# MLP borders of a two-layer decoder: elementwise work on VectorE in place of GpSimd, and other PSUM banks for early products

## The chip, the cores and the metric

The kernel runs on one core of a Trainium2 chip. Five engines of the core work side by side, each through its own instructions in a fixed order: TensorE (PE in the rows; PEld is its weight load), VectorE (DVE), ScalarE (ACT), GpSimd (POOL) and SyncE (SP), which here only issues DMAs. They wait for each other through semaphores. The metric is the device time of one execution in microseconds (us), lower is better.

## The reference

Two layers of a decoder on x of 1024 tokens by 1024 features, all in float32. A layer has three residual steps; the third, the MLP, is the one at issue:

```python
def rms_norm(x, g):
    y = x * lax.rsqrt(jnp.mean(x * x, axis=-1, keepdims=True) + NORM_EPS)
    return y * g

for l in range(2):
    h = rms_norm(x, norm_mix_pre[l])
    ...                       # four mixers side by side, then w_out
    x = x + rms_norm(mixed, norm_mix_post[l])
    xa = cross_attention(rms_norm(x, norm_xa_pre[l]), ...)
    x = x + rms_norm(xa, norm_xa_post[l])
    hid = jnp.square(jax.nn.relu(rms_norm(x, norm_mlp_pre[l]) @ mlp_w1[l]))   # 1024 -> 4096
    x = x + rms_norm(hid @ mlp_w2[l], norm_mlp_post[l])                       # 4096 -> 1024
```

## The kernel before, in words

**Float32 products in three passes.** An operand is split into a high part (ScalarE's cast, L197) and the rest (VectorE's subtraction, L198): `wh`/`wl` and `hT` for the first matrix, `ao`/`bo` for the second, from raw tiles `wraw`, `araw` and `braw` that DMAs bring. A product is then three matmuls, L210 to L212 or L246 to L248. So each operand goes through ScalarE and VectorE once before TensorE can use it.

**Seven products in place of eight.** Both MLP products are cut into blocks of two by two and use a scheme of Strassen's kind: seven block products on sums and differences of blocks. For the first matrix the weights' sums S1 to S4 are made by L1471 to L1474 on GpSimd, and the tokens' sums T1 to T4 in `mlp_turn`, which transposes the normed tiles 4 to 7 (the tiles of the second half of the tokens) and subtracts or adds the transposes of tiles 0 to 3, as high and low parts: L1416 and L1425 (VectorE) take the high part, L1417 and L1426 (GpSimd) the low part. T-sums of the second matrix's blocks are made in `sums` (L1630 to L1639, GpSimd).

**First matrix.** Sixteen groups g of weights. `p1` and `p2` are a group's first two products; those of g = 0, 1, 2 need tiles 0 to 3 only and are run early, among the tail of cross attention (L309 adds its output to x, from a PSUM bank) and `mlp_turn`. `group` then runs the other products (and p1, p2 of the later groups), adds them up (L1531 to L1544, from PSUM, L1535 on GpSimd) and applies relu squared (L1499). The hidden blocks go to DRAM and come back as `araw`.

**Second matrix.** Blocks b = 0 to 4 of the hidden dimension. For b = 0 to 3 the seven products are added to accumulators `acc` (L1731 for b = 0, L1733 after it, four each), and in b = 3 `fold` adds accumulators to each other (L1670, 14 instructions a layer on GpSimd), which ends the scheme. Two orders of the products differ in where the folds come: after b = 3's P2, P5, P7 and P3. The last block is done as plain products by token tile (L1753); `part` takes the sum of squares (L1682, ScalarE) and multiplies by the norm's gain (L1683, GpSimd); `row` sums the squares (L1688), takes the power (`rstd`, L255 and L256 on GpSimd) and adds the row to the residual x (L1692). In the first layer the next layer's norm follows tile by tile (L275, L277, transposes L287); in the last layer this is the end of the kernel.

**What orders the work.** The functions are generators that are interleaved by hand; every engine runs its instructions in program order, and a tile's buffer is given to the next tile of its tag only when its last reader is done. PSUM has three pools: d (2 banks), u (4) and r (2).

Of the kernel before, what the change touches and what calls it, by code (L numbers as in the profile page):

```python
# [86 lines left out]
class Kern:  # L87
# [1303 lines left out]
    def mlp_turn(self, xs, tt, pst, X):  # L1391

        V, A, P, T = self.nc.vector, self.nc.scalar, self.nc.gpsimd, self.nc.tensor
        cs = slice(128 * (tt % 4), 128 * (tt % 4) + 128)
        if tt == 4:
            pair = lambda tag: [tuple(self.slot(tag, (128, 2, 512), F32R, name="hT") for _ in range(2)) for _ in range(2)]
            X[1] = {name: pair(tag) for name, tag in (("B22", "h"), ("T1", "h"), ("T2", "r"), ("T3", "r"), ("T4", "r"))}
        x = X[1]
        pt = []
        for b in range(2):  # L1400
            pt.append(self.psum(pst, (128, 4, 128), "pt"))
            for j in range(4):
                k = 4 * b + j
                T.transpose(pt[b][:, j, :], xs[:, k * 128:(k + 1) * 128], self.ident)
        b12, b22 = pt
        f, t2 = (xs[:, 512 * i:512 * i + 512].rearrange("p (k c) -> p k c", k=4) for i in range(2))
        two = lambda t, j: t[:, 2 * j:2 * j + 2]
        low = [tuple(t[:, :, cs] for t in X[0][j]) for j in range(4)]

        def split(name, src):  # L1410
            for j in range(2):
                h, lo = (t[:, :, cs] for t in x[name][j])
                self.split(h, lo, two(src, j))

        for j in range(2):
            V.tensor_tensor(two(f, j), two(b12, j), low[j][0], ALU.subtract)  # L1416
            P.tensor_tensor(two(f, j), two(f, j), low[j][1], ALU.subtract)  # L1417
        split("B22", b22)
        V.tensor_tensor(t2, b22, f, ALU.subtract)
        split("T1", f)  # L1420
        A.copy(f, b12)
        V.tensor_tensor(f, b22, f, ALU.subtract)
        split("T2", t2)
        for j in range(2):
            V.tensor_tensor(two(t2, j), low[2 + j][0], two(t2, j), ALU.subtract)  # L1425
            P.tensor_tensor(two(t2, j), two(t2, j), low[2 + j][1], ALU.add)  # L1426
        split("T3", f)
        split("T4", t2)

    def mlp(self, l, hT, gpost, gpre, xin, xout, dst, nxt):  # L1430
# [24 lines left out]
        def weights(g, raw=None):  # L1455

            if raw is None:
                raw = [self.slot("wr", name="wraw") for _ in range(2)]
                for i in range(2):
                    self.dma(raw[i], W[l, 2 * g + i])  # L1460
                yield
            if g not in ops:
                ops[g] = dict(zip(("A11", "A12"), pair(raw[0])))
            if g:
                yield
            o = ops[g]
            b = self.slot(("wh", "wl")[g % 2], (128, 2, 512), F32R, name="wb")
            self.split(b[:, 0], b[:, 1], raw[1][:, 512:1024])
            o["A22"] = tuple(b[:, i].rearrange("p (k c) -> p k c", k=4) for i in range(2))
            (a11, a12), (a21, a22) = ((r[:, 0:512], r[:, 512:1024]) for r in raw)  # L1470
            P.tensor_tensor(a22, a21, a22, ALU.add)  # L1471
            P.tensor_tensor(a21, a11, a21, ALU.subtract)  # L1472
            P.tensor_tensor(a11, a22, a11, ALU.subtract)
            P.tensor_tensor(a12, a12, a11, ALU.subtract)  # L1474
            yield
            yield
            o["S3"], o["S1"] = pair(raw[1])
            yield
            o["S2"], o["S4"] = pair(raw[0])
            yield  # L1480

        def product(g, tag, w, x):
            (wh, wl), xs = ops[g][w], X[x]
            ps = self.psum(tag)
            for k in range(4):
                xh, xl = xs[k // 2]
                self.mm3(ps, wh[:, k], wl[:, k], xh[:, k % 2], xl[:, k % 2], k == 0, k == 3)
                yield
            return ps
# [10 lines left out]

        def p1(g):
            s = gs[g] = dict(A=two("r", "ma"))
            ps = yield from product(g, "d", "A11", "B11")
            A.copy(s["A"][:, 0], ps)

        def p2(g):
            s = gs[g]
            s["B"] = two("g" if g < 2 else "x", "mb")
            ps = yield from product(g, "d", "A12", "B21")
            V.tensor_tensor(s["B"][:, 0], ps, s["A"][:, 0], ALU.add)  # L1510
            sq(s["B"][:, 0], g < NE)

# [110 lines left out]

        def sums(b, name):

            for u in range(len(blocks[b])):
                r = lambda n: rawB[b, n][u]
                if name == "T2":
                    b11, b12, b22 = (r(n) for n in ("B11", "B12", "B22"))
                    P.tensor_tensor(b11, b12, b11, ALU.subtract)  # L1630
                    rawB.setdefault((b, "T1"), []).append(b11)
                    t = self.slot("g", name="t2")
                    P.tensor_tensor(t, b22, b11, ALU.subtract)
                elif name == "T3":
                    t = r("B12")
                    P.tensor_tensor(t, r("B22"), t, ALU.subtract)
                else:
                    t = r("B21")
                    P.tensor_tensor(t, t, r("T2"), ALU.subtract)  # L1639
                rawB.setdefault((b, name), []).append(t)  # L1640

        def ahead():
# [24 lines left out]
        def fold(*pairs):  # L1667
            for to, of in pairs:
                for k in range(2):
                    P.tensor_tensor(acc[to][k], acc[to][k], acc[of][k], ALU.add)  # L1670

        folds = {"P2": (("P2", "P1"), ("P6", "P1")), "P5": (("P5", "P6"), ("P4", "P6")), "P7": (("P3", "P5"),),
                 "P3": (("P5", "P7"), ("P4", "P7"))}
# [3 lines left out]
        def part(tt, c, t, pst="d"):  # L1677

            if tt not in ssq:
                ssq[tt] = self.small([128, 2], "ssm", 5)  # L1680
            jk = self.psum(pst, name="junk")
            A.activation(jk, t, AF.Square, scale=D ** -0.5, accum_out=ssq[tt][:, c:c + 1])  # L1682
            P.tensor_tensor(t, t, gp[:, halves[c]], ALU.mult)  # L1683

        def row(tt, x):
            ss = ssq[tt]
            s1 = self.small([128, 1], "ssq", 3)
            V.scalar_tensor_tensor(s1, ss[:, 0:1], EPS, ss[:, 1:2], ALU.add, ALU.add)  # L1688
            r = self.rstd(s1)
            for p, sl in zip((("P2", "P3"), ("P4", "P5"))[tt // 4], halves):  # L1690
                t = y(p, tt % 4)
                V.scalar_tensor_tensor(x[:, sl], t, r, x[:, sl], ALU.mult, ALU.add)  # L1692
                if last and tt >= NT - 2:
                    self.dma(xout[tt][:, sl], x[:, sl])
            if not (last and tt >= NT - 2):
                self.dma(xout[tt], x)
            if not last:
                late.append((self.scaled(x, gn), tt))
# [321 lines left out]
```

## Time and profile before

| | us |
|---|---|
| three runs | 3330.42, 3341.13, 3345.55 (median 3341.13) |
| profiled execution, device time | 3333.72 |
| its span in the trace | 3331.9 |

The profiled execution granted TensorE 0.968 of its clock in the mean. The rows below are from this one execution, so its own time, 3333.72 us, is what sums of durations are held against. Rows of a timeline have the start in us from the span's start, the duration, engine, line, operation, output and inputs, and in brackets the idle time ahead of it on its engine with what ended it; "x2" stands for two like instructions in a row, whose durations are then taken together.

### The profile page before, as it was taken

How to read it: one execution, taken by the hardware profiler on the slowest of the kernel's cores; microseconds unless marked ns; L12 is line 12 of the kernel's file. 1: busy time of each engine (PE TensorE's matmuls, PEld its weight loads, DVE VectorE, ACT ScalarE, POOL GpSimd, SP SyncE). 2: the span in 40 equal slices, each digit the busy share in tenths (PEclk: the TensorE clock that was granted, in tenths of full speed). 3: DMA queues.
4: the chain of work that ended last, by engine and by line, in shares of the span. 5: the costliest groups of instructions: out<-in, count | busy, mean ns of one | idle time of the engine just before them, and what ended most of it. 6: DMA issues, size and time to landing. Idle time of an engine off the chain costs nothing. (4 is left out here: it accounts for less than half of the span.)

```text
span 3331.9 us, 46885 instructions
## 1 busy us (share of the span) xinstructions
PE 3150.6 (95%) x17696; PEld 2539.5 (76%) x17696; DVE 2085.0 (63%) x3316; ACT 1305.9 (39%) x2404; POOL 998.5 (30%) x762
## 2 busy tenths in 40 slices
PE   8999999999989998999799999899999899989997
PEld 6767777878867886887677777778788778878876
DVE  4457568364466667789634765673644676677894
ACT  5344444343443223433333454433434432234332
POOL 1000122010016776337410002110100168763374
PEclk9989999999999999999999999888999999999998
DMA  4323473252333445544333324622523334445433
GB/s 173 112 71 93 118 206 105 77 186 76 102 115 120 152 152 182 190 147 130 122 120 107 108 90 115 182 93 88 172 74 104 114 119 158 153 181 184 150 124 114
DMA packets 230850, 431.40 MB, mean 129 GB/s; under 512 B 59968, under 2 KB 109248, under 8 KB 230624
## 3 DMA queue, kind: packets, MB, share of 16 engines
q1 hardware_dynamic: 223968, 411.42, 37.3%
q0 software_dynamic: 6656, 16.98, 2.0%
q8 instruction: 140, 2.29, 0.3%
q14 instruction: 86, 0.70, 0.1%
HBM read 296.61 MB, written 131.69 MB: 129 GB/s over the span
## 5 line engine op out<-in xcount | busy, mean ns | idle before, releaser
L210 PE MATMUL p<-hT,wh 128*128 128x512 f32 x1536 | 616.4, 401 | 18.9 <-DVE x L309 10.7
L212 PE MATMUL p<-hT,wl 128*128 128x512 f32 x1536 | 606.2, 395 | 8.1 <-DVE wl L198 7.9
L211 PE MATMUL p<-hT,wh 128*128 128x512 f32 x1536 | 606.2, 395 | 0.0
L198 DVE TENSOR_TENSOR wl<-wraw,wh 128x1024 fp32r<-128x1024 f32 (+1 forms) x230 | 282.1, 1227 | 348.6 <-ACT wh L197 347.7
L197 ACT CAST wh<-wraw 128x1024 fp32r<-128x1024 f32 (+1 forms) x230 | 240.0, 1044 | 487.6 <-POOL wraw L1472 182.3
L246 PE MATMUL p<-bo,ao 128*128 128x512 f32 x912 | 361.1, 396 | 39.8 <-DVE mb L1544 25.1
L210 PEld LDWEIGHTS p<-hT,wh 128*128 128x128 f32 x1536 | 292.0, 190 | 95.2 <-issue 12.3
L247 PE MATMUL p<-bo,ao 128*128 128x512 f32 x912 | 358.7, 393 | 0.0
L248 PE MATMUL p<-bo,ao 128*128 128x512 f32 x912 | 358.5, 393 | 0.1
L212 PEld LDWEIGHTS p<-hT,wl 128*128 128x128 f32 x1536 | 291.3, 190 | 76.1 <-DVE wl L198 15.0
L211 PEld LDWEIGHTS p<-hT,wh 128*128 128x128 f32 x1536 | 292.0, 190 | 57.6 <-issue 0.7
L246 PEld LDWEIGHTS p<-bo,ao 128*128 128x128 f32 x912 | 174.0, 191 | 79.6 <-DVE mb L1544 26.0
L198 DVE TENSOR_TENSOR ao<-araw,ao 128x1024 fp32r<-128x1024 f32 x106 | 194.2, 1834 | 24.6 <-ACT ao L197 24.6
L246 PE MATMUL p<-wh,mt 128*128 128x512 f32 x512 | 204.2, 399 | 1.4 <-ACT junk L301 0.9
L248 PEld LDWEIGHTS p<-bo,ao 128*128 128x128 f32 x912 | 173.4, 190 | 37.7 <-DVE bo L198 0.9
L247 PEld LDWEIGHTS p<-bo,ao 128*128 128x128 f32 x912 | 173.9, 191 | 35.9
L248 PE MATMUL p<-wl,mt 128*128 128x512 f32 x512 | 200.9, 393 | 0.3 <-DVE wl L198 0.3
L247 PE MATMUL p<-wh,mt 128*128 128x512 f32 x512 | 200.9, 393 | 0.0
L198 DVE TENSOR_TENSOR bo<-braw,bo 128x1024 fp32r<-128x1024 f32 x92 | 158.6, 1726 | 59.0 <-ACT bo L197 49.7
L197 ACT CAST bo<-braw 128x1024 fp32r<-128x1024 f32 x92 | 96.1, 1050 | 224.1 <-PE p L247 128.0
L256 POOL TENSOR_TENSOR rs<-ssq,neghalf 128x1 f32<-128x1 f32 x48 | 27.1, 564 | 519.2 <-DVE ssq L303 508.9
L197 ACT CAST ao<-araw 128x1024 fp32r<-128x1024 f32 x106 | 110.9, 1050 | 88.9 <-DMA araw<-hd 88.3
(385 smaller groups left out, 6485.7 us busy)
## 6 DMA issues: line engine op xcount, KB each, us to landing
araw<-hd SPq DMA_DIRECT2D x106, 512.0 KB, 4.0
x<-x SPq DMA_DIRECT2D x80, 512.0 KB, 3.4
wraw<-in_mlp_w SPq DMA_DIRECT2D x68, 512.0 KB, 3.5
braw<-in_mlp_w SPq DMA_DIRECT2D x64, 512.0 KB, 4.8
wraw<-in_w_fm SPq DMA_DIRECT2D x32, 512.0 KB, 3.8
pj<-spl SPq DMA_DIRECT2D x64, 256.0 KB, 2.0
hd<-mb SPq DMA_DIRECT2D x64, 256.0 KB, 2.5
hd<-mc SPq DMA_DIRECT2D x64, 256.0 KB, 2.0
```

The costliest lines, as they stand in the source:

```text
L197: self.nc.scalar.copy(h, src)
L198: self.nc.vector.tensor_tensor(lo, src, h, ALU.subtract)
L210: mm(ps, wh, xl, start=first, stop=False)
L211: mm(ps, wh, xh, start=False, stop=False)
L212: mm(ps, wl, xh, start=False, stop=last)
L246: mm(ps, xl, wh, start=first, stop=False)
L247: mm(ps, xh, wh, start=False, stop=False)
L248: mm(ps, xh, wl, start=False, stop=last)
L256: P.tensor_tensor(r, ss, self.neghalf[:, 0:k], ALU.pow)
```

## The change

Six edits in the MLP, all of them about who does a step or where its result lies:

1. In `mlp_turn` L1417 and L1426 (the low parts) go from GpSimd to VectorE.
2. The weights' block sums L1471 to L1474 go to VectorE for group 0; the other fifteen groups keep GpSimd.
3. In `sums` the T-sums of block b = 0 of the second matrix go to VectorE; b = 1 to 3 keep GpSimd.
4. The folds go to VectorE.
5. `part` no longer multiplies by the gain. `row` multiplies y by the rstd and the gain in one VectorE instruction, and adds it to x in a second one.
6. p1 and p2 of the groups g = 0, 1, 2 take their PSUM banks from pool u rather than from d.

```diff
--- before.py
+++ after.py
@@ -1414,7 +1414,7 @@
 
         for j in range(2):
             V.tensor_tensor(two(f, j), two(b12, j), low[j][0], ALU.subtract)
-            P.tensor_tensor(two(f, j), two(f, j), low[j][1], ALU.subtract)
+            V.tensor_tensor(two(f, j), two(f, j), low[j][1], ALU.subtract)
         split("B22", b22)
         V.tensor_tensor(t2, b22, f, ALU.subtract)
         split("T1", f)
@@ -1423,7 +1423,7 @@
         split("T2", t2)
         for j in range(2):
             V.tensor_tensor(two(t2, j), low[2 + j][0], two(t2, j), ALU.subtract)
-            P.tensor_tensor(two(t2, j), two(t2, j), low[2 + j][1], ALU.add)
+            V.tensor_tensor(two(t2, j), two(t2, j), low[2 + j][1], ALU.add)
         split("T3", f)
         split("T4", t2)
 
@@ -1468,10 +1468,11 @@
             self.split(b[:, 0], b[:, 1], raw[1][:, 512:1024])
             o["A22"] = tuple(b[:, i].rearrange("p (k c) -> p k c", k=4) for i in range(2))
             (a11, a12), (a21, a22) = ((r[:, 0:512], r[:, 512:1024]) for r in raw)
-            P.tensor_tensor(a22, a21, a22, ALU.add)
-            P.tensor_tensor(a21, a11, a21, ALU.subtract)
-            P.tensor_tensor(a11, a22, a11, ALU.subtract)
-            P.tensor_tensor(a12, a12, a11, ALU.subtract)
+            E = P if g else V
+            E.tensor_tensor(a22, a21, a22, ALU.add)
+            E.tensor_tensor(a21, a11, a21, ALU.subtract)
+            E.tensor_tensor(a11, a22, a11, ALU.subtract)
+            E.tensor_tensor(a12, a12, a11, ALU.subtract)
             yield
             yield
             o["S3"], o["S1"] = pair(raw[1])
@@ -1500,13 +1501,13 @@
 
         def p1(g):
             s = gs[g] = dict(A=two("r", "ma"))
-            ps = yield from product(g, "d", "A11", "B11")
+            ps = yield from product(g, "u" if g < NE else "d", "A11", "B11")
             A.copy(s["A"][:, 0], ps)
 
         def p2(g):
             s = gs[g]
             s["B"] = two("g" if g < 2 else "x", "mb")
-            ps = yield from product(g, "d", "A12", "B21")
+            ps = yield from product(g, "u" if g < NE else "d", "A12", "B21")
             V.tensor_tensor(s["B"][:, 0], ps, s["A"][:, 0], ALU.add)
             sq(s["B"][:, 0], g < NE)
 
@@ -1623,20 +1624,21 @@
 
         def sums(b, name):
 
+            E = P if b else V
             for u in range(len(blocks[b])):
                 r = lambda n: rawB[b, n][u]
                 if name == "T2":
                     b11, b12, b22 = (r(n) for n in ("B11", "B12", "B22"))
-                    P.tensor_tensor(b11, b12, b11, ALU.subtract)
+                    E.tensor_tensor(b11, b12, b11, ALU.subtract)
                     rawB.setdefault((b, "T1"), []).append(b11)
                     t = self.slot("g", name="t2")
-                    P.tensor_tensor(t, b22, b11, ALU.subtract)
+                    E.tensor_tensor(t, b22, b11, ALU.subtract)
                 elif name == "T3":
                     t = r("B12")
-                    P.tensor_tensor(t, r("B22"), t, ALU.subtract)
+                    E.tensor_tensor(t, r("B22"), t, ALU.subtract)
                 else:
                     t = r("B21")
-                    P.tensor_tensor(t, t, r("T2"), ALU.subtract)
+                    E.tensor_tensor(t, t, r("T2"), ALU.subtract)
                 rawB.setdefault((b, name), []).append(t)
 
         def ahead():
@@ -1667,7 +1669,7 @@
         def fold(*pairs):
             for to, of in pairs:
                 for k in range(2):
-                    P.tensor_tensor(acc[to][k], acc[to][k], acc[of][k], ALU.add)
+                    V.tensor_tensor(acc[to][k], acc[to][k], acc[of][k], ALU.add)
 
         folds = {"P2": (("P2", "P1"), ("P6", "P1")), "P5": (("P5", "P6"), ("P4", "P6")), "P7": (("P3", "P5"),),
                  "P3": (("P5", "P7"), ("P4", "P7"))}
@@ -1680,7 +1682,6 @@
                 ssq[tt] = self.small([128, 2], "ssm", 5)
             jk = self.psum(pst, name="junk")
             A.activation(jk, t, AF.Square, scale=D ** -0.5, accum_out=ssq[tt][:, c:c + 1])
-            P.tensor_tensor(t, t, gp[:, halves[c]], ALU.mult)
 
         def row(tt, x):
             ss = ssq[tt]
@@ -1689,7 +1690,8 @@
             r = self.rstd(s1)
             for p, sl in zip((("P2", "P3"), ("P4", "P5"))[tt // 4], halves):
                 t = y(p, tt % 4)
-                V.scalar_tensor_tensor(x[:, sl], t, r, x[:, sl], ALU.mult, ALU.add)
+                V.scalar_tensor_tensor(t, t, r, gp[:, sl], ALU.mult, ALU.mult)
+                V.tensor_tensor(x[:, sl], t, x[:, sl], ALU.add)
                 if last and tt >= NT - 2:
                     self.dma(xout[tt][:, sl], x[:, sl])
             if not (last and tt >= NT - 2):
```

Lines behind L1471 stand one or two further down in the changed file: L1499 is L1500 there, L1535 L1536, L1544 L1545, L1630 L1632, L1670 L1672, L1733 L1735.

VectorE at the start of the MLP, where tile 7 (`xsn_9465`) goes through `mlp_turn` and group 0's last raw weights (`wraw_9174`) are split into `wl_9657`. Before:

```order
L1419 TENSOR_TENSOR xsn_9465<-pt_9615,xsn_9465 128x512
L198 TENSOR_TENSOR hT_9308<-xsn_9465,hT_9307 128x2x128
L198 TENSOR_TENSOR wl_9657<-wraw_9174,wh_9656 128x1024
L1422 TENSOR_TENSOR xsn_9465<-pt_9615,xsn_9465 128x512
L198 TENSOR_TENSOR hT_9310<-xsn_9465,hT_9309 128x2x128
L198 TENSOR_TENSOR hT_9312<-xsn_9465,hT_9311 128x2x128
L1425 TENSOR_TENSOR xsn_9465<-hT_8851,xsn_9465 128x256
L1425 TENSOR_TENSOR xsn_9465<-hT_8853,xsn_9465 128x256
L198 TENSOR_TENSOR hT_9314<-xsn_9465,hT_9313 128x2x128
L198 TENSOR_TENSOR hT_9316<-xsn_9465,hT_9315 128x2x128
L198 TENSOR_TENSOR hT_9318<-xsn_9465,hT_9317 128x2x128
L198 TENSOR_TENSOR hT_9320<-xsn_9465,hT_9319 128x2x128
```

After the change:

```order
L1422 TENSOR_TENSOR xsn_9465<-pt_9615,xsn_9465 128x512
L198 TENSOR_TENSOR hT_9310<-xsn_9465,hT_9309 128x2x128
L198 TENSOR_TENSOR hT_9312<-xsn_9465,hT_9311 128x2x128
L1425 TENSOR_TENSOR xsn_9465<-hT_8851,xsn_9465 128x256
L1425 TENSOR_TENSOR xsn_9465<-hT_8853,xsn_9465 128x256
L1426 TENSOR_TENSOR xsn_9465<-xsn_9465,hT_8852 128x256
L1426 TENSOR_TENSOR xsn_9465<-xsn_9465,hT_8854 128x256
L198 TENSOR_TENSOR hT_9314<-xsn_9465,hT_9313 128x2x128
L198 TENSOR_TENSOR hT_9316<-xsn_9465,hT_9315 128x2x128
L198 TENSOR_TENSOR hT_9318<-xsn_9465,hT_9317 128x2x128
L198 TENSOR_TENSOR hT_9320<-xsn_9465,hT_9319 128x2x128
L198 TENSOR_TENSOR wl_9657<-wraw_9174,wh_9656 128x1024
```

The split `wl_9657` stood ahead of tile 7's L1422; now it stands behind all of that tile's instructions, among which are the two L1426 of edit 1.

VectorE at the border between the two matrices, in the last group (g = 15), whose products end in `ma_11698`, `mc_11743` and `mb_11725`; `braw`, `t` and `bo` are block 0 of the second matrix. Before:

```order
L1534 TENSOR_TENSOR ma_11698<-p_11778,ma_11698 128x512
L198 TENSOR_TENSOR ao_11893<-araw_11851,ao_11892 128x1024
L1536 TENSOR_TENSOR mc_11743<-mc_11743,ma_11698 128x512
L198 TENSOR_TENSOR bo_11956<-t_2372_11886,bo_11955 128x1024
L1539 TENSOR_TENSOR mc_11743<-p_11794,mc_11743 128x512
L1540 TENSOR_TENSOR ma_11698<-p_11794,ma_11698 128x512
L1499 SCALAR_TENSOR_TENSOR mc_11743<-mc_11743 128x1024
L1544 TENSOR_TENSOR mb_11725<-p_11810,ma_11698 128x512
```

After the change:

```order
L1535 TENSOR_TENSOR ma_11698<-p_11778,ma_11698 128x512
L1632 TENSOR_TENSOR braw_11696<-braw_11758,braw_11696 128x1024
L1537 TENSOR_TENSOR mc_11743<-mc_11743,ma_11698 128x512
L1635 TENSOR_TENSOR t_2372_11886<-braw_11741,braw_11696 128x1024
L1540 TENSOR_TENSOR mc_11743<-p_11794,mc_11743 128x512
L1541 TENSOR_TENSOR ma_11698<-p_11794,ma_11698 128x512
L1500 SCALAR_TENSOR_TENSOR mc_11743<-mc_11743 128x1024
L1545 TENSOR_TENSOR mb_11725<-p_11810,ma_11698 128x512
L198 TENSOR_TENSOR ao_11893<-araw_11851,ao_11892 128x1024
L1500 SCALAR_TENSOR_TENSOR mb_11725<-mb_11725 128x512
L1638 TENSOR_TENSOR braw_11758<-braw_11741,braw_11758 128x1024
```

L1632 and L1635 (edit 3) have come in, and the splits `ao_11893` and `bo` of t, which stood ahead of L1545 (L1544 before), now stand behind it.

ScalarE in the last blocks, the casts for the last products of b = 3 and for the plain phase; `bo_13828` and `bo_13845` take buffers of accumulators that the folds read last. Before:

```order
L197 CAST ao_13704<-araw_13622 128x1024
L197 CAST bo_13828<-braw_13690 128x1024
L197 CAST bo_13845<-braw_13784 128x1024
L197 CAST ao_13723<-araw_13641 128x1024
L197 CAST ao_13790<-araw_13708 128x1024
```

After the change:

```order
L197 CAST bo_13763<-braw_13048 128x1024
L197 CAST ao_13723<-araw_13641 128x1024
L197 CAST ao_13790<-araw_13708 128x1024
L197 CAST bo_13828<-braw_13690 128x1024
L197 CAST bo_13845<-braw_13784 128x1024
```

The casts `ao_13723` and `ao_13790` stood behind the two `bo`; now they stand ahead of them.

## Rows read from the trace of the kernel before

**Rows 1.** The page, part 1: busy time of each engine, share of the span, instructions.
```profile
PE 3150.6 (95%) x17696; PEld 2539.5 (76%) x17696; DVE 2085.0 (63%) x3316; ACT 1305.9 (39%) x2404; POOL 998.5 (30%) x762
```

**Rows 2.** The waits of PE: line waiting, releaser, us in total, times, longest.
```profile
PE p L246 <- DVE mb L1544: 25.1, 2, 13.3
PE p L246 <- DVE ao L198: 13.0, 4, 4.3
PE p L210 <- DVE x L309: 10.7, 4, 3.1
```

**Rows 3.** Windows: us, busy PE, PEld, DVE, ACT, POOL (x instructions), granted clock, DMA.
```profile
975.00:1036.00 61.00, 47.90 (x189) 35.40 (x188) 50.37 (x93) 33.03 (x73) 29.88 (x31) 0.92 0.24 82
1503.00:1606.00 103.00, 94.86 (x408) 76.88 (x407) 88.81 (x68) 34.84 (x35) 69.08 (x22) 0.98 0.37 114
1606.00:1690.00 84.00, 67.89 (x307) 54.77 (x306) 59.42 (x85) 34.87 (x85) 34.09 (x40) 0.92 0.42 144
3171.00:3274.00 103.00, 96.38 (x407) 77.99 (x406) 88.86 (x68) 34.78 (x35) 68.74 (x22) 0.97 0.31 103
```

**Rows 4.** Window of tile ao, then of bo, 1503 to 1606: PE, PEld, DVE, ACT.
```profile
1503.00:1606.00 103.00, 94.86 (x408) 76.88 (x407) 34.26 (x17) 17.63 (x17) 0.98 0.37 114
...
1503.00:1606.00 103.00, 94.86 (x408) 76.88 (x407) 37.06 (x18) 18.59 (x18) 0.98 0.37 114
```

**Rows 5.** Groups by line on POOL: busy us, mean ns of one, idle before.
```profile
L1670 POOL TENSOR_TENSOR acc<-acc,acc 128x1024 f32<-128x1024 f32 x28 | 86.6, 3112 | 43.8 <-DVE acc L1733 26.2 <-issue 17.6
L1683 POOL TENSOR_TENSOR acc<-acc,gain 128x512 f32<-128x512 f32 x32 | 42.0, 1324 | 60.2 <-ACT junk L1682 60.2
```

**Rows 6.** Timeline of DVE, then POOL, 1005 to 1026: start, us, instruction.
```profile
1005.79 2.29 DVE L198 TENSOR_TENSOR wl<-wraw,wh 128x1024 fp32r<-128x1024 f32 x1
1019.67 0.75 DVE L1425 TENSOR_TENSOR xsn<-hT,xsn 128x256 f32<-128x256 f32 x2
...
1025.21 1.29 POOL L1471 TENSOR_TENSOR wraw<-wraw 128x512 f32<-128x512 f32 x1 [2.83 <-DVE wb L198]
```

**Rows 7.** Timeline 1316 to 1328 of POOL, then DVE, then PE.
```profile
1318.04 3.20 POOL L1633 TENSOR_TENSOR t<-braw,braw 128x1024 f32<-128x1024 f32 x1
1321.20 1.71 POOL L1535 TENSOR_TENSOR mc<-mc,ma 128x512 f32<-128x512 f32 x1
...
1316.28 2.77 DVE L198 TENSOR_TENSOR ao<-araw,ao 128x1024 fp32r<-128x1024 f32 x1
1318.97 2.82 DVE L1536 TENSOR_TENSOR mc<-mc,ma 128x512 f32<-128x512 f32 x1
1322.35 1.65 DVE L198 TENSOR_TENSOR bo<-t,bo 128x1024 fp32r<-128x1024 f32 x1 [0.56 <-ACT bo L197]
1325.12 2.17 DVE L1499 SCALAR_TENSOR_TENSOR mc<-mc 128x1024 f32<-128x1024 f32 x1
1327.22 0.68 DVE L1544 TENSOR_TENSOR mb<-p,ma 128x512 f32<-128x512 f32 x1
...
1327.95 0.80 PE L246 MATMUL p<-bo,ao 128*128 128x512 f32 x1 [13.34 <-DVE mb L1544]
```

**Rows 8.** Timeline 1587 to 1590 of ACT; 1580 to 1591 of DVE.
```profile
1587.51 1.04 ACT L197 CAST bo<-braw 128x1024 fp32r<-128x1024 f32 x1 [11.91 <-POOL acc L1670]
...
1580.80 1.21 DVE L198 TENSOR_TENSOR bo<-braw,bo 128x1024 fp32r<-128x1024 f32 x1
1581.94 1.27 DVE L1733 TENSOR_TENSOR acc<-p,acc 128x512 f32<-128x512 f32 x2
1589.54 1.23 DVE L198 TENSOR_TENSOR ao<-araw,ao 128x1024 fp32r<-128x1024 f32 x1 [6.33 <-ACT ao L197]
```

**Rows 9.** Timeline 1627 to 1632 of DVE, then PE; 3312 of POOL.
```profile
1627.29 2.28 DVE L277 SCALAR_TENSOR_TENSOR xsn<-x,rs,gain 128x1024 f32<-128x1024 f32 x1 [1.92 <-POOL rs L256]
...
1631.86 1.09 PE L287 MATMUL pt<-ident,xsn 128*128 128x128 f32 x4 [5.81 <-DVE hT L198]
...
3312.98 2.52 POOL L1683 TENSOR_TENSOR acc<-acc,gain 128x512 f32<-128x512 f32 x2 [2.97 <-ACT junk L1682]
```

## The prediction

> **What bounds the kernel now.** The page's first line comes first: TensorE is busy for 95% of the span, VectorE for 63%, GpSimd for 30% [rows 1]. In the mean nothing but TensorE counts, and 95% leaves at most 181 us of TensorE's idle time over the whole kernel to fight for. So the question is where it is idle, and who ends that. The list of TensorE's waits names three releasers that belong to the MLP alone [rows 2]: a product of the second matrix that waits for L1544 (25.1 us in two waits, one a layer), products of the last blocks that wait for a VectorE subtraction `ao` (13.0 us), and early products that wait for L309 to give up a bank (10.7 us). In the plain phase transposes of the next layer's normed tiles wait for `hT`, up to 5.81 us [rows 9]. None of these releasers is GpSimd. But all of them are VectorE instructions that themselves come late, and the windows show what else runs then: in the start of the MLP (975 to 1036) TensorE is busy for 47.90 of 61 us, in the last blocks (1503 to 1606) for 94.86 of 103 with VectorE at 88.81 and GpSimd at 69.08, in the plain phase of the first layer (1606 to 1690) for 67.89 of 84 [rows 3]. These idle pieces, 13.1, 8.1 and 16.1 us, with the two waits of about 12.5 us for L1544, are what the change can touch in a layer.
>
> **Why GpSimd matters at all.** A VectorE split of 128x1024 takes 1.21 us when GpSimd is still (1.14 from its start to the next one's) [rows 8] and 2.29 us in a stretch where GpSimd works [rows 6]. In the window of the last blocks the 17 subtractions `ao` and 18 `bo` took 34.26 and 37.06 us [rows 4]; at 1.21 us they would take 42.4, so 29 us of the 88.81 are stretch. Instructions that read PSUM (0.68 us for L1544 while GpSimd ran) [rows 7] show none. So an instruction taken from GpSimd costs VectorE its own time and gives back stretch.
>
> **The change, place by place** (times of layer 1; layer 2 has the same places).
>
> *Border between the two matrices.* TensorE waits 13.34 us up to 1327.95 for L1544, which ends at 1327.9 [rows 7]. Followed back: L1499 took 2.17 us at 1325.12, ahead of it stood the split `bo<-t` at 1322.35, which waited until GpSimd's L1633 had made t at 1321.24; L1536 took 2.82 us beside L1633; and GpSimd's L1535 stood behind L1633 until 1321.20. After the change the row order on VectorE is L1632, L1537, L1635, L1540, L1541, L1500, L1545, with the split of t behind L1545. From 1316.3, where `ao` started, that is L1632 1.2, L1537 0.7 (up to 1.3 beside GpSimd's L1536, which no longer queues), L1635 1.2, two of 0.68, L1500 1.2 (half of a stretched 2.17) and L1545 0.68: 6.3 to 6.9 us, so 1322.6 to 1323.2 in place of 1327.9. The gain is 5 us, in layer 2 as much: **-10**. Bounds: 0 if the block's load or its splits are late next (the splits of `ao` now stand behind L1545), -25 if the whole wait went.
>
> *Folds.* 14 folds a layer, 28 in all, take 3.11 us each on GpSimd [rows 5]; on VectorE I price one as a split of the same shape, 1.14 us from start to start, so 14 x 1.14 = 16 us are added. The folds are 43.6 of the window's 69.08 us of GpSimd, so of the 29 us of stretch 18 go. VectorE's need falls from 88.8 to about 87 us in a stage in which TensorE needs 94.9. The late chain goes as well: ScalarE's `bo` at 1587.51 waited 11.91 us for a GpSimd fold, since it takes that fold's buffer, and VectorE's `ao` at 1589.54 stood 6.33 us behind it [rows 8]. In the new ScalarE order those two `ao` casts come ahead of the two `bo`, and the folds they wait for end some 4 us sooner. Following VectorE's new order with these prices, each `ao` and `bo` of the last products is ready 3 to 7 us before TensorE wants it. So nearly all idle time goes: 8.1 us, and the clock's share (granted 0.98 over 94.9 us of work, 1.9 us), 10.0 together; in layer 2 (3171 to 3274) 6.6 us idle and 0.97 granted, 2.9 us, 9.5 together [rows 3]. I take 9.5 a layer: **-19**. Bounds: -20, and +16 a layer if the folds lie wholly on the path (below).
>
> *Row weights.* GpSimd's multiplies L1683 (1.32 us in the mean) stand ahead of the row's rstd on GpSimd; L277 of the next layer took 2.28 us beside one [rows 5, 9]. Now a row costs VectorE two more additions of 0.6 and loses one or two multiplies on the path (1.3 to 2.6 us; I take 1.9) and about a microsecond of stretch (L277 as the splits above): 1.9 + 1.0 - 1.2 = 1.7 us a tile. At four tiles of the first layer's plain phase TensorE waits for the transposed tile by over 2 us, the first time 5.81 [rows 9]; 4 x 1.7 is **-7** of the 16.1 us idle there. Bounds 0 and -16. In the tail the last tile's two multiplies take 2.52 us ahead of rstd [rows 9]; the square sum covers 0.8 of it, and two additions (1.2) come behind: 0.5 less a tile, over the last six, which run in a chain: **-3** (bounds 0 and -4).
>
> *Start of the MLP.* Here VectorE gains work: per layer 16 subtractions and additions of 128x256 (two take 0.75 us, start to start 0.34) [rows 6] and four block sums of 128x512, priced as L1733 (0.6, two in 1.27) [rows 8]: 16 x 0.34 + 4 x 0.6 = 7.8 us. GpSimd is rid of them; I put the stretch given back at 4 us, half of the rate in the last blocks (29 us in 69), as many VectorE instructions here read PSUM. VectorE is busy for 50.37 of 61 us [rows 3], so the net 4 us land partly in its idle time. What is late next: in the new order the last split that reads group 0's raw weights stands eleven rows later, behind all of tile 7's subtractions (0.6 + 0.67 + 0.67 + 0.67 + 1.34 = 4 us), and group 1's weights are loaded into those buffers, so GpSimd's sums of group 1, which start at 1025.21 after a wait for `wb` [rows 6], come later by what isn't slack; I put 2.5 us on the path. The other banks let two early products start at once rather than after L309 (10.7 us in four waits [rows 2]), but TensorE then waits for the same transposes and weights, which VectorE makes: nothing. So +2.5 a layer: **+5**. Bounds -10 (the bank waits go) and +10 (all added work on the path).
>
> Other instructions keep their order within a few rows; the folds' accumulators and tiles lie in the same buffers.
>
> **Sum.** -10 - 19 - 7 - 3 + 5 = -34 us. The profiled execution took 3333.7 us, so 3300. The median of the runs shown is 3341.1, 7.4 above it, which would give 3307. I forecast between the two: **3304 us**.
>
> **Rivals.**
> 1. *VectorE becomes the bound in the last blocks, evenly matched:* a product needs four splits (4.6 us), four adds from PSUM (2.4) and up to four folds (4.6), 11.6 us, while TensorE spends some 11.2 us on one (48 of the window's 408 matmuls, 94.9 x 48 / 408 [rows 3]). For it: VectorE is at 86% there already. Against it: only four of seven products carry folds, and the others leave a lead. Then the last blocks gain nothing, the start costs 5 a layer, and -10 - 7 - 3 + 10 = -10: 3324 to 3331, no difference to be told.
> 2. *Slower: the folds stall the banks.* Two folds in a row (2.3 us) stand on VectorE ahead of the add that frees a PSUM bank. From the point where VectorE has no lead over TensorE when a fold comes up, each fold delays TensorE by its 1.14 us: 16 us a layer lost in place of 9.5 gained, 51 us worse than the forecast, 3355. Against it: VectorE idles 6.33 us in this stage [rows 8], and its need of 87 lies under 94.9. The Trainium skill speaks for this rival: "Perfetto Trace Analysis", Optimizing Scalar/DVE Operations, advises to take work off a saturated VectorE, even to GpSimd, though it adds that the two share a port and this may not help. By its first half the move is the wrong way; the stretch measured here is its second half.
> 3. *More gain:* the bank waits do go (-5 a layer in the start in place of +2.5) and the plain phase is freed by -12: 3304 - 20 = 3284.
> 4. *Borders hidden anyway:* what VectorE frees earlier is then late by loads or ScalarE; half the gain, 3320, within the forecast's own range.
>
> **How the numbers follow.** About 0.5% (17 us) is what a measurement of this kernel can tell from no change. Forecast and rival 4: 0.61 together, own range 3290 to 3322; rival 1: 0.18; rival 2: 0.08; rival 3: 0.13. Faster by over 0.5% (below 3324): 0.61 less the 0.02 at its upper edge, and 0.13, so 0.72; within: 0.20; slower: 0.08. The range reaches down to rival 3 and up into rival 1, and leaves out about 2 in 10: 3283 to 3327.
>
> **What would show it.** TensorE's wait for L1545 falls from 12.5 to about 7.5 us in each layer; its waits for `ao` nearly vanish; splits in the last blocks average 1.3 to 1.6 us where they average 2.0 now; VectorE stays under 90 of 103 us there. In the start of the MLP the waits for L309 go, and later waits for transposes or weights take their place, with TensorE's idle time about 15 in place of 13. Waits of the next layer's transposes shrink by about 7. Wrong it would be if the waits for `ao` turn into waits for L1735 (a bank that comes free late behind folds), or if group 1's weights come later than 2.5 us in the start.

## The result and the profile after

The changed kernel took 3298.85 us in the median of six runs (3289.44 to 3312.21), the kernel before 3335.78 (3319.6 to 3347.08): a ratio of 0.9895, 95% interval 0.9858 to 0.9933, so 35 us or 1.05% faster. Forecast were 3304 us, 3283 to 3327.

The profiled execution of the changed kernel is 3308.01 us, its span 3306.2, only 25.7 less than before. Its page, part 1, beside [rows 1]:

```profile
PE 3148.4 (95%) x17696; PEld 2545.9 (77%) x17696; DVE 2096.9 (63%) x3424; ACT 1306.2 (40%) x2404; POOL 804.1 (24%) x654
```

The waits of TensorE (us in total, times, longest), beside [rows 2]: L1545 costs 15.7 in place of 25.1 us, the waits for `ao` and for L309 are gone from the list, and waits for transposes and weight splits of the start have come:

```profile
PE p L246 <- DVE mb L1545: 15.7, 2, 8.5
PE p L212 <- DVE wl L198: 17.1, 8, 4.9
PE pt L1404 <- DVE xsn L1422: 14.4, 6, 5.6
PE p L248 <- DVE bo L198: 3.9, 2, 2.0
```

The windows of the changed kernel that lie between the same matmuls as stages of before: start, last blocks, plain phase, last blocks of layer 2 (columns as in [rows 3]). Below them the last blocks and the plain phase of before, cut at the same matmuls:

```profile
983.40:1047.20 63.80, 47.27 (x190) 36.24 (x189) 52.92 (x113) 32.98 (x73) 10.52 (x11) 0.87 0.23 79
1509.90:1606.30 96.40, 94.46 (x417) 77.88 (x417) 91.59 (x85) 36.79 (x38) 25.65 (x8) 1.00 0.40 128
1606.30:1676.70 70.40, 61.60 (x298) 49.53 (x297) 56.20 (x99) 33.82 (x84) 12.68 (x24) 1.00 0.46 161
3156.40:3253.20 96.80, 94.84 (x412) 77.99 (x411) 90.20 (x83) 35.79 (x36) 25.67 (x8) 0.98 0.33 110
```

The kernel before:

```profile
1503.10:1608.20 105.10, 96.96 (x416) 78.64 (x415) 90.31 (x70) 35.89 (x36) 69.08 (x22) 0.98 0.37 113
1608.20:1690.10 81.90, 65.79 (x297) 53.03 (x296) 57.82 (x83) 33.82 (x84) 34.09 (x40) 0.92 0.43 146
```

**A measure that one profile can carry.** Every trace has the same 17696 matmuls. I take the start of the same matmul (counted in TensorE's order, which differs inside the start and the plain phase of some runs, but not at the cuts) in two traces; the time between two of them is a stage. The stages are cut, by the times of before, at 975, 1304, 1332, 1503, 1608 and 1690 us in layer 1, and at 2644, 2972, 3000, 3171, 3275 and the end in layer 2. "Rest" is all the other time, in which no run here differs in code. Difference to before in us:

| kernel | start 1, 2 | border 1, 2 | last blocks 1, 2 | plain 1 | tail | rest |
|---|---|---|---|---|---|---|
| changed | +2.6, +3.4 | -4.2, -5.5 | -8.8, -7.1 | -11.5 | -3.8 | +9.4 |
| blocksums_back | +3.7, +3.8 | -4.3, -4.2 | -8.8, -8.8 | -10.7 | -3.9 | +2.7 |
| turn_back | +6.9, +8.1 | -4.7, -6.1 | -8.8, -8.8 | -11.5 | -4.2 | -8.8 |
| banks_back | +4.4, +4.0 | -5.4, -6.5 | -8.8, -8.7 | -11.5 | -3.7 | +6.3 |
| start_back | -0.1, +0.2 | -2.9, -4.7 | -8.8, -7.2 | -11.5 | -4.2 | -3.1 |
| start_half | +0.2, +0.6 | -3.7, -4.7 | -7.2, -7.2 | -11.5 | -4.2 | +0.5 |
| sums_back | +2.9, +3.7 | -0.1, +0.1 | -7.2, -8.8 | -11.5 | -4.2 | +6.6 |
| folds_back | +3.5, +3.4 | -2.7, -5.3 | 0.0, +0.1 | -9.0 | -4.2 | +13.2 |
| folds_only | -0.1, +0.1 | +0.6, -1.0 | -8.8, -7.2 | -0.7 | +0.3 | -9.6 |
| folds_noise | +3.7, +3.3 | -2.9, -4.4 | +6.2, +6.1 | -9.5 | -4.1 | +13.2 |
| folds_double | +3.2, +3.5 | -3.5, -5.7 | -0.9, -1.6 | -10.8 | -3.7 | -2.1 |
| folds_noise_free | +2.5, +2.7 | -4.8, -4.5 | +9.7, +9.9 | -11.0 | -4.2 | -10.9 |
| row_back | +2.6, +2.8 | -4.1, -3.9 | -8.8, -8.8 | -1.3 | 0.0 | +3.9 |

A stage repeats within 2 us where its code is the same (the border within 3), and the rest moves by 24 us from run to run. (The blocks between border and last blocks differ by under 0.5 us everywhere and are left out.) The changed kernel's stages sum to -35 us; +9.4 in the rest hides a quarter of it in this one profile.

### The profile page after: what moved, and what is told of

Read it like the earlier page. It is cut to its first block, busy times and chain, and to the rows that moved or that the text cites. A ratio compares the mean times of both kernels' runs of the same rounds, so it can differ in the third digit from the quotient of the medians.

```text
span 3306.2 us, 46802 instructions
## 1 busy us (share of the span) xinstructions
PE 3148.4 (95%) x17696; PEld 2545.9 (77%) x17696; DVE 2096.9 (63%) x3424; ACT 1306.2 (40%) x2404; POOL 804.1 (24%) x654
## 5 line engine op out<-in xcount | busy, mean ns | idle before, releaser
L212 PE MATMUL p<-hT,wl 128*128 128x512 f32 x1536 | 604.4, 394 | 17.3 <-DVE wl L198 17.1
L246 PE MATMUL p<-bo,ao 128*128 128x512 f32 x912 | 357.8, 392 | 15.7 <-DVE mb L1545 15.7
L198 DVE TENSOR_TENSOR ao<-araw,ao 128x1024 fp32r<-128x1024 f32 x106 | 172.4, 1626 | 14.3 <-ACT ao L197 14.2
L198 DVE TENSOR_TENSOR bo<-braw,bo 128x1024 fp32r<-128x1024 f32 x92 | 146.6, 1597 | 42.5 <-ACT bo L197 42.5
```

What stands on the lines that cost most here:

```text
L198: self.nc.vector.tensor_tensor(lo, src, h, ALU.subtract)
L212: mm(ps, wl, xh, start=False, stop=last)
L246: mm(ps, xl, wh, start=first, stop=False)
```

## The experiments

All edits are to the changed kernel, except in folds_only. V is VectorE, P GpSimd.

### The start of the MLP

**blocksums_back**

```diff
-            E = P if g else V      # in weights()
+            E = P
```

> Measured by the start stage, between the two matmuls that stand at 975 and 1036 us in the trace of before (61.0 us there; 63.8 and 64.3 us in the two layers of the changed kernel). Theory: the four block sums on VectorE stand ahead of the split that TensorE then waits 4.90 us for, so with them back on GpSimd that wait goes and the stage falls by 2 to 3 us a layer, to about 61.3. Rival: the 16 subtractions of the tiles are the cost, the split is only late in their wake, and the stage stays at 63.5 to 64.5.

Up to the matmul at 1036 the stage is 63.9 and 63.7 us: nothing saved. The wait for the split shrinks from 4.90 to 3.92 us only. The theory fell and the rival's number came; start_back below shows that the block sums cost as much when they alone are on VectorE.

**turn_back**

```diff
-            V.tensor_tensor(two(f, j), two(f, j), low[j][1], ALU.subtract)
+            P.tensor_tensor(two(f, j), two(f, j), low[j][1], ALU.subtract)
-            V.tensor_tensor(two(t2, j), two(t2, j), low[2 + j][1], ALU.add)
+            P.tensor_tensor(two(t2, j), two(t2, j), low[2 + j][1], ALU.add)
```

> Same stage. Theory (the block sums are the cost): about 63 us, at most 1 us less than the changed kernel's 63.8 and 64.3, since what VectorE is spared it loses again beside GpSimd. Rival (the 16 subtractions are the cost): 61 us or less, and TensorE's wait of 5.56 us for a transposed tile shrinks below 3 us.

63.8 and 63.7 us up to that matmul, and 4.1 and 5.4 more than before between it and 1304. The rival fell. The theory's number nearly came, but blocksums_back had shown that the block sums are not the whole cost, and the loss behind the matmul was in neither. Timeline of PE, then of ACT, of this run:

```profile
1046.22 0.80 PE L210 MATMUL p<-hT,wh 128*128 128x512 f32 x1 [5.41 <-ACT mc L1527]
...
1044.64 1.04 ACT L197 CAST wh<-wraw 128x1024 fp32r<-128x1024 f32 x1 [2.50 <-POOL wraw L1475]
1045.59 0.58 ACT L1527 COPY mc<-p 128x512 f32<-128x512 f32 x1
```

The same in the changed kernel:

```profile
1058.59 0.50 PE L210 MATMUL p<-hT,wh 128*128 128x512 f32 x1 [1.26 <-ACT mc L1527]
...
1057.01 1.05 ACT L197 CAST wh<-wraw 128x1024 fp32r<-128x1024 f32 x1 [4.88 <-POOL wraw L1473]
1057.96 0.58 ACT L1527 COPY mc<-p 128x512 f32<-128x512 f32 x1
1060.58 1.06 ACT L197 CAST wh<-wraw 128x1024 fp32r<-128x1024 f32 x1 [2.04 <-POOL wraw L1475]
```

TensorE waits 5.41 us for the copy `mc`, which in turn_back stands on ScalarE behind the cast that waits for GpSimd's L1475 of group 2; in the changed kernel it stands ahead of that cast, and the wait is 1.26 us. What an edit costs here depends on the order that comes with it on a third engine.

**banks_back**

```diff
-            ps = yield from product(g, "u" if g < NE else "d", "A11", "B11")   # and A12
+            ps = yield from product(g, "d", "A11", "B11")
```

> Same stage. Theory (banks are worth nothing, since TensorE waits for the same tiles and weights later): within 0.7 us of the changed kernel, 63.2 to 65, with the waits for L309 of about 10 us in all back and the waits for transposes and weights shorter by as much. Rival (the banks do save, and hide a larger loss by VectorE's added work): 66 us or more a layer.

Up to the matmul at 1036 the stage is 62.9 and 62.2 us, 0.9 and 2.2 less than in the changed kernel and below the theory's range; the rival fell. Over the stage up to 1304 this run is 1.8 and 0.6 us longer, within the 2 us by which a stage scatters. That excess comes behind the matmul at 1036: ScalarE has the order of turn_back here, and TensorE waits 4.1 and 3.9 us for the copy `mc`, 1.3 in the changed kernel. So it is not shown that the banks by themselves are worth anything. The waits for L309 came back, those for L1422 and `wl` fell from 31.5 to 6.7 us (total of the two lines):

```profile
PE p L210 <- DVE x L309: 11.6, 4, 3.3
PE pt L1404 <- DVE xsn L1422: 5.7, 6, 1.8
PE p L212 <- DVE wl L198: 1.0, 2, 0.5
PE p L210 <- ACT mc L1527: 8.0, 2, 4.1
```

**start_back** (both edits of blocksums_back and turn_back)

> Both moves of the start undone, banks kept. Theory: the stage is back at 61 us or a little below, 3 us a layer less than in the changed kernel, so some 6 us less in all: about 3293 beside a median of 3299 for the changed kernel. Rival (the banks by themselves are worth the 10 us of waits for L309): 56 to 58 us a layer, 12 to 16 us less in all, about 3285.

The start is as long as before (-0.1, +0.2), 2.7 and 3.2 us a layer less than in the changed kernel; the rival fell. The median of four runs is 3296.67 us (about 3293 expected), ratio to before 0.9901 (0.9872 to 0.9931): a gain of 6 us can't be told from the changed kernel's 0.9895 that way, the stages alone show it. Of TensorE's waits those for `wl` fall, from 17.1 to 10.7 us, and those for L1422 stay (14.4 in the changed kernel):

```profile
PE pt L1404 <- DVE xsn L1422: 13.5, 4, 5.5
PE p L212 <- DVE wl L198: 10.7, 10, 2.0
```

Four of these kernels make a square. Up to the matmul at 1036, against start_back, the subtractions alone on VectorE (blocksums_back) cost 2.7 and 2.3 us, the block sums alone (turn_back) 2.6 and 2.4, both together (the changed kernel) 2.5 and 3.0. So either move by itself costs all of it, and the second adds nothing that can be told; why is open.

**start_half** (start_back, with tiles 4 and 5 on VectorE)

```diff
+            (V if tt < 6 else P).tensor_tensor(two(f, j), two(f, j), low[j][1], ALU.subtract)   # and t2
```

> The subtractions of tiles 4 and 5 alone are on VectorE, those of tiles 6 and 7 and the block sums of group 0 are back on GpSimd, the early products keep the u banks. Start stage as above, up to the matmul at 1304. Theory (the cost is VectorE work that stands ahead of the splits of group 0's weights, which is that of tiles 6 and 7 and the block sums): as with both moves undone or up to 1 us better, 60 to 61.5 us, 3 us a layer less than in the changed kernel, about 3293 in all. Rival (every tile costs alike): halfway, 62 to 63 us.

+0.2 and +0.6: like start_back, so the subtractions of tiles 4 and 5 cost nothing that can be told; the median of four runs is 3299.91 us (about 3293 expected), ratio 0.9884 (0.9849 to 0.9919). blocksums_back differs from it by the subtractions of tiles 6 and 7 alone, and is 3.5 and 3.2 us longer: these are the cost while the block sums are on GpSimd.

### The border and the folds

**sums_back**

```diff
-            E = P if b else V      # in sums()
+            E = P
```

> The T-sums of block 0 are back on GpSimd. Measured between the matmuls that stand at 1304 and 1332 us (2972 and 3000) in the trace of before, where the changed kernel is 4.2 and 5.5 us shorter. Theory (L1633 on GpSimd holds up the split of t, L1536 and their stretch, and with them L1545): all of it comes back, the wait for L1545 is 12 to 13.5 us again. Rival (VectorE's new order, with the splits behind L1545, does it by itself): at most 2 us come back.

The border is as before (-0.1, +0.1), and the wait for L1545 is 12.7 us a layer again: the T-sums made all of that gain.

```profile
PE p L246 <- DVE mb L1545: 25.4, 2, 13.2
```

**folds_back**

```diff
-                    V.tensor_tensor(acc[to][k], acc[to][k], acc[of][k], ALU.add)
+                    P.tensor_tensor(acc[to][k], acc[to][k], acc[of][k], ALU.add)
```

> Measured by the fold stage, between the matmuls that stand at 1503 and 1608 us (3171 and 3275 in layer 2) in the trace of before; the changed kernel is 8.8 and 7.2 us shorter there. Theory (GpSimd's folds cost stretch and a late chain): with the folds back on GpSimd all of it comes back, +7 to +9 us a layer, and TensorE waits 12 us or more for ao again. Rival (the plain phase's and the other edits' orders made it): less than 3 us a layer comes back.

The last blocks are as before to 0.1 us, and the wait for `ao` is back, at 11.5 us, a little under the 12 expected:

```profile
PE p L246 <- DVE ao L198: 11.5, 4, 4.3
```

**folds_only** (the folds' edit made to the kernel before)

> The kernel before with the folds on VectorE and nothing else. Theory (the places are independent but for what passes from the folds to the plain phase): the fold stage is 8 to 9 us shorter than before in layer 1 and 7 in layer 2, and the plain phase of layer 1, whose multiplies stay on GpSimd, up to 1 us either way; in all some 16 us less than before, about 3318. Rival (the fold stage needs what the T-sums of block 0 or the early start save): under 5 us a layer.

-8.8 and -7.2 by itself: the theory. (In all 3307.31 us, of which -9.6 are the rest.)

**folds_noise**

```diff
                     V.tensor_tensor(acc[to][k], acc[to][k], acc[of][k], ALU.add)
+                    P.tensor_tensor(scr, acc[to][k], acc[to][k], ALU.mult)   # rearrange of both inputs left out
```

> The folds stay on VectorE; for each, GpSimd multiplies an accumulator by itself into a scratch tile that nobody reads, which takes the time and the port of a fold but holds no buffer that the next operands need. Same stage. Theory (stretch: VectorE has about 87 us of work for 90 us): splits of 128x1024 are stretched again from 1.2 to about 2 us in the mean, VectorE would need 100 us or more, and the stage grows by 8 to 16 us a layer over the changed kernel. Rival (the gain came from the buffers that come free earlier and from the casts' order, not from stretch): at most 3 us a layer.

15.0 and 13.2 us over the changed kernel, as the theory says. But here GpSimd also reads an accumulator, so the next run frees that.

**folds_noise_free**

```diff
+                    P.tensor_copy(scr[:, k:k + 1], acc[to][k][:, 0, 0:1])   # behind each fold
+            for _ in range(2 * len(pairs)):                                 # behind a product's folds
+                P.tensor_tensor(scr, scr, scr, ALU.mult)
```

> As the run in which GpSimd squared an accumulator beside each fold, which lost 15.0 and 13.2 us a layer in the fold stage, but 5.1 us a layer of that were waits for an accumulator that GpSimd still read. Here GpSimd copies one column of the folded accumulators and then squares a scratch tile of its own, once for each fold, behind all folds of a product. Theory (stretch alone): waits for accumulators under 1 us, and still 7 to 12 us a layer more than the changed kernel. Rival (the hold of the accumulators made that loss, and the gain of the change came from its end): at most 4 us a layer.

18.5 and 17.0 us over the changed kernel, more than either theory gave. The last blocks of this run, all instructions, then those of `ao` and of `bo` (DVE is the third pair of the first row and of the others):

```profile
1492.70:1607.50 114.80, 101.68 (x416) 82.26 (x415) 110.64 (x85) 36.64 (x37) 69.70 (x36) 0.93 0.34 107
...
1492.70:1607.50 114.80, 101.68 (x416) 82.26 (x415) 33.89 (x17) 17.86 (x17) 0.93 0.34 107
...
1492.70:1607.50 114.80, 101.68 (x416) 82.26 (x415) 38.54 (x18) 18.80 (x18) 0.93 0.34 107
```

The rows of `ao` and `bo` in the same stage of the changed kernel:

```profile
1509.90:1606.30 96.40, 94.46 (x417) 77.88 (x417) 27.31 (x17) 17.89 (x17) 1.00 0.40 128
...
1509.90:1606.30 96.40, 94.46 (x417) 77.88 (x417) 27.08 (x18) 18.70 (x18) 1.00 0.40 128
```

The same 35 splits take 72.4 us here and 54.4 in the changed kernel: 18 us of stretch, and VectorE is busy for 110.64 of 114.8 us. On TensorE 7.2 of the 18.5 us show as its own work (101.68 us at a granted clock of 0.93, 94.46 at 1.00), the rest as waiting. The expectation misread one row: the waits for `acc`, 10.0 us here too, are for VectorE's own additions that free a bank, not for GpSimd's hold.

**folds_double**

```diff
+                    V.tensor_tensor(acc[to][k], acc[to][k], acc[to][k], ALU.max)
                     V.tensor_tensor(acc[to][k], acc[to][k], acc[of][k], ALU.add)
```

> Each fold on VectorE comes with a second VectorE instruction of its shape that leaves its accumulator as it is (a maximum of it with itself): 16 us more a layer and no GpSimd. Same stage. Theory (VectorE is already at its bound there, idle for under 1 us between 1540 and 1596): of the 16 us 12 to 16 land on the path in each layer, since there is only 2 to 4 us of slack. Rival (a lead of 3 to 7 us before each product, as in the prediction): 16 less 7, at most 9 us a layer.

The stage grew by 7.9 and 5.5 us, but not out of 16. Of the 14 added instructions a layer 7 ran 2 to 41 us ahead of the stage, in blocks that got no longer by it. Windows of this run, all instructions, then the added ones:

```profile
1505.30:1609.50 104.20, 97.23 (x416) 78.59 (x415) 99.95 (x92) 36.69 (x38) 23.76 (x8) 0.98 0.38 117
...
1505.30:1609.50 104.20, 12.26 (x7) 0.98 0.38 117
```

VectorE's busy time in the stage rose by 8.4 us (91.59 to 99.95), in layer 2 by 8.9, and 7.9 and 5.5 of that landed on the path. So the rival's number came for another reason than the rival gives: what VectorE has in hand is half a microsecond in layer 1 and 3.4 in layer 2. The other runs with folds on VectorE fit. In layer 1 the stage is VectorE's busy time and 4 to 5 us in each: 96.40 and 91.59 in the changed kernel, 104.20 and 99.95 here, 111.30 and 107.35 in folds_noise, 114.80 and 110.64 in folds_noise_free. With the folds on GpSimd it is 105.10 and 90.31 (before).

### The row weights

**row_back**

```diff
+            P.tensor_tensor(t, t, gp[:, halves[c]], ALU.mult)          # in part()
-                V.scalar_tensor_tensor(t, t, r, gp[:, sl], ALU.mult, ALU.mult)
-                V.tensor_tensor(x[:, sl], t, x[:, sl], ALU.add)
+                V.scalar_tensor_tensor(x[:, sl], t, r, x[:, sl], ALU.mult, ALU.add)
```

> The gain's multiply is back on GpSimd, the row is one VectorE instruction. Measured from the matmul that stands at 1608 us in before to the one at 1690, and from that at 3275 to the end. Theory: the plain phase of layer 1 grows by 10 to 12 us, and the tail by 3 to 4. Rival (part of that gain came from folds that end earlier and so let the plain phase start with all operands ready): only 3 to 7 us in the plain phase.

10.2 of the plain phase's 11.5 us and all of the tail's 3.8 come back; 1.3 stay: the theory held. From the other side, without the folds' edit the plain phase gains 9.0. TensorE's own work in this phase is 65.8 us before, 65.9 here, 65.5 in folds_back and 61.6 in the changed kernel, so the 4.2 us that it fell by came only with both edits.

## Why the prediction was right, step by step

*Sum.* -34 was forecast for the stages, -35 measured. That the two are so close is luck in part: the folds gave 3 us less than their term, the row weights 5 more.

*Border, -10: -9.7.* The wait for L1545 is 7.85 us a layer, forecast was 7.5. Timeline of DVE, then PE, of the changed kernel:

```profile
1327.07 1.22 DVE L1632 TENSOR_TENSOR braw<-braw,braw 128x1024 f32<-128x1024 f32 x1
1328.20 1.76 DVE L1537 TENSOR_TENSOR mc<-mc,ma 128x512 f32<-128x512 f32 x1
1332.21 1.21 DVE L1500 SCALAR_TENSOR_TENSOR mc<-mc 128x1024 f32<-128x1024 f32 x1
1333.35 0.68 DVE L1545 TENSOR_TENSOR mb<-p,ma 128x512 f32<-128x512 f32 x1
...
1334.08 0.79 PE L246 MATMUL p<-bo,ao 128*128 128x512 f32 x1 [8.49 <-DVE mb L1545]
```

From L1632 to the end of L1545 it is 6.96 us, forecast were 6.3 to 6.9. L1537 took 1.76 beside GpSimd's half, above the 1.3 I allowed, and L1500 1.21 in place of 2.17 [rows 7].

*Folds, -19: -15.9.* The price was right: the splits lost 16.9 us of stretch (71.3 us in [rows 4], 54.4 now; 18 forecast). But the folds took 18.1 us in place of 16, and VectorE's busy time, cut at the same matmuls, went from 90.3 to 91.6 us, where I had it fall by 2. So the stretch given back paid for the folds, and the gain shows as an end of waiting: VectorE's idle time in the stage fell from 14.8 to 4.8 us, and the late chain of [rows 8] is gone. How the 8.8 us divide between stretch and late chain is not shown. TensorE is now busy for 94.46 of 96.4 us at a granted clock of 1.00, so little is left to gain; one wait of 1.94 us is left, for a `bo` of t. The size was taken a little high: that new wait was not in it, and in layer 2 the granted clock stayed at 0.98. The step that each `ao` and `bo` is ready 3 to 7 us early was wrong: this `bo` comes late, and folds_double leaves VectorE a lead of 0.5 and 3.4 us. Rivals 1 and 2 did not come, but they were nearer than the prediction had them. The Trainium skill's caution in "Perfetto Trace Analysis", Optimizing Scalar/DVE Operations, that moving work from VectorE to GpSimd may not help as they share a port, fits this: folds_back loses 8.8 and 7.2 us by that move. No run here shows the port itself.

*Row weights, -7 and -3: -11.5 and -3.8.* TensorE's idle time in the plain phase fell from 16.1 to 8.8 us, the 7 forecast. The other 4.2 us are its own work, 65.8 us at a granted clock of 0.92 and 61.6 at 1.00; row_back and folds_back show that this came only with both edits. I had counted such a share for the last blocks and left it out here. In the tail TensorE runs its last 173 matmuls without a gap in both traces, and the time behind the last one fell from 17.2 to 13.4 us. A tile now takes 5.56 us from rstd to rstd, about 6.0 before:

```profile
3289.66 0.55 POOL L256 TENSOR_TENSOR rs<-ssq,neghalf 128x1 f32<-128x1 f32 x1 [5.01 <-DVE ssq L1689]
3295.22 0.55 POOL L256 TENSOR_TENSOR rs<-ssq,neghalf 128x1 f32<-128x1 f32 x1 [5.00 <-DVE ssq L1689]
```

*Start of the MLP, +5: +6.0.* The size was right by luck, since the place was not. I had put the loss on the last split of group 0's raw weights and the GpSimd sums behind it. Those sums start 11.2 us later than before, but so do TensorE's matmuls at that point, and the two waits behind them are 1.03 and 0.53 us in both traces: the sums hold up no more than they did. The time went earlier. Timeline of PE, then DVE:

```profile
1000.58 1.94 PE L1404 MATMUL pt<-ident,xsn 128*128 128x128 f32 x8 [5.56 <-DVE xsn L1422]
1021.27 0.79 PE L212 MATMUL p<-hT,wl 128*128 128x512 f32 x1 [4.90 <-DVE wl L198]
...
1016.19 0.75 DVE L1426 TENSOR_TENSOR xsn<-xsn,hT 128x256 f32<-128x256 f32 x2
1018.20 0.68 DVE L1473 TENSOR_TENSOR wraw<-wraw,wraw 128x512 f32<-128x512 f32 x1
1019.40 0.68 DVE L1474 TENSOR_TENSOR wraw<-wraw,wraw 128x512 f32<-128x512 f32 x1
1020.00 1.21 DVE L198 TENSOR_TENSOR wl<-wraw,wh 128x1024 fp32r<-128x1024 f32 x1
```

With the early products out of the way TensorE waits once, 5.56 us, for a transposed tile, where it waited in pieces before; this wait is there without the two moves too (5.5 in start_back), so it only stands in for the waits for L309. What the moves cost is in the waits for `wl`, 4.90 us here, ahead of which VectorE has tile 6's additions and two block sums. It is shown that the stage gets longer with turn_back, stays within its scatter with blocksums_back, and gets shorter with both; that ScalarE's order does it is shown only for the loss behind 1036 in turn_back and banks_back.

## What to carry to other kernels

Where VectorE splits two-input tiles beside GpSimd, price a GpSimd instruction at its stretch on VectorE too: here a 3.1 us fold cost VectorE 1.2 us of stretch, about what doing the fold itself costs, and it came late besides [rows 8]. Compare stages between the same instructions of two traces when the edits are worth microseconds and the runs differ by tens; then count the idle time and the clock's share separately. Undo moves together as well as singly: here either of two moves cost as much as both, and the order on a third engine cost 4 us more in a run that undid one of them. When a probe adds instructions, count in the trace how many ran where they were meant to: in folds_double half of them did not.

## What was not expected of the hardware

The scatter between runs lies outside the MLP: the rest moved from -10.9 to +13.2 us with the same code. It is not waiting. In all 14 traces TensorE is idle for 77 to 82 us of the rest, but its own work there takes from 2181 to 2203 us. The granted clock goes with it. The traces have two levels of it, 2.4 and 1.2 GHz: the three with a rest below -8 spend 95 to 101 us of the rest at the lower one, the three above +9 spend 139 to 146. Between the plain phase of layer 1 and the MLP of layer 2, where the code is the same, folds_back (+13.2) and then folds_only (-9.6) show 33.5 and 34.4 us of TensorE's idle time, and 927 and 915 us of work:

```profile
1688.70:2649.20 960.50, 927.05 (x5990) 740.05 (x5989) 517.88 (x1088) 398.11 (x828) 90.29 (x138) 0.96 0.36 113
...
1676.10:2625.60 949.50, 915.09 (x5990) 729.96 (x5989) 518.98 (x1090) 397.83 (x829) 90.36 (x139) 0.97 0.36 114
```

Why the clock falls for longer in one run than in the next, with the same waits, stays open.

In the start of the MLP the granted clock fell from 0.92 to 0.87 [rows 3] while TensorE's idle time rose by 3.4 us, much of it in the one wait of 5.56 us. Its busy time there did not rise (47.90 and 47.27 us), so these rows show no time lost by that fall.
